# Hymba decoder layer on one core: a wide last block of the expert down part, and another order of the closing stage

## The chip, the core and the metric

The kernel runs on one core of a Trainium2 chip. The time is device microseconds of one execution, from runs of the whole kernel; lower is better. In the profile, PE is TensorE's matmuls (PEld its weight loads), DVE is VectorE, ACT is ScalarE, POOL is GpSimd, SP is SyncE, which here only issues DMA.

## The reference

One decoder layer over 256 tokens of width 2048, all in float32:

```python
h = x + concat(forgetting_attention(...), gelu(gate) * rg_lru(...)) @ w_out
hn = rms_norm(h, ffn_norm)                    # top-1 of 4 groups, top-2 of 8 experts in it
for e in range(32):
    hid = silu(hn @ w_gate[e]) * (hn @ w_up[e])          # 2048 -> 256
    out += (hid @ w_down[e]) * comb[:, e:e+1]            # 256 -> 2048
h = h + out
gate = sigmoid(rms_norm(h, ple_norm) @ w_ple_gate)       # 2048 -> 2048
h = h + gate * (p @ w_ple_up)
```

## The kernel before

A float32 matmul whose result must be close is done as three matmuls of fp32r halves: ScalarE copies a 128x512 chunk to its high half (`uh`, L179), VectorE subtracts to the low half (`ul`, L180), and TensorE sums high by high, high by low and low by high.

**Weights** stream from HBM through a ring of slots of 1 MB each (`slot()`, three pools, 12 slots in the last stages). SyncE issues the transfers in program order; each waits until its slot's last reader is through. Where a weight is an expert's, SyncE first loads the expert's number from a table (L965).

**Experts, first part.** Tokens are sorted by expert. A 0/1 matrix `sel01` (two halves of 256 sorted places, written by `select(0)` and `select(1)`, L836 to L843) gathers their rows on TensorE (`gather`, L859 and L860), and `stage1` (L900) multiplies by gate and up weights. A loop over i = 0 to 15 (L1043) takes the four experts whose slots were filled ahead: step i gathers piece i + 1, copies it, and runs stage 1 on piece i; i = 0 to 7 need the first half of `sel01`, i = 8 to 15 (whose first gather runs in step 7) the second. In between VectorE sorts the experts (`by_rank`, `by_count`). GpSimd subtracts for the splits of h (L577). Then seven rounds of four experts follow, bound by the transfer of w_gu.

**Experts, second part, with the closing gate.** Output columns come in BLOCKS of 512, 512, 512, 256 and 256. For each block, nine rounds r of two or four experts: `down(r, b)` fetches their w_down columns (one transfer for each expert, L966), multiplies (`y`, L970), copies y to `yh` (L974) and subtracts to `yl` (L975); `scatter` (L981) sums it into `o`, one round behind. After a block `o` is added to h (L1211), h is transposed (L1129) and split into `th`, `tl` (L1133, L1134), and squares are summed (L1138). In the next block's even rounds a `gate_step(b - 1, n)` multiplies these columns by chunk n of w_ple_gate (w_pg; L1174 to L1176) and adds to z (L1183). After the last block four gate steps remain, of two 128-row pieces each. The closing steps of a tile are the sigmoid on ScalarE (L1186), the product with u = p @ w_ple_up (L1187), the sum with h (L1188), and the store (L1189); for n = 0 and 1 GpSimd takes product and sum, for n = 2 and 3 VectorE.

**Order.** In this last stage SyncE and TensorE follow program order (`manual_schedule`); the scheduler orders VectorE and ScalarE.

Of the kernel before, what the change touches and what calls it, by code (L numbers as in the profile page):

```python
# [10 lines left out]
F32 = mybir.dt.float32  # L11
# [28 lines left out]
BLOCKS = ((0, 512), (512, 512), (1024, 512), (1536, 256), (1792, 256))  # L40
# [22 lines left out]
def hymba_layer_kernel(ctx, tc, x, xT, gains, w_in, w_f, rnn_v, w_gates, qk_g, b_f, w_out,  # L63
# [980 lines left out]
    for i in range(16):  # L1044
# [15 lines left out]
        if i == 0:  # L1060
            by_rank()
        elif i == 1:
            by_rank_rest()
        elif i == 2:
            token_weights()
        elif i == 3:
            token_weights_rest()
        elif i < 8:
            next(counts, None)
        if i == 6:  # L1070
            select(1)
            for r in range(pairs, 2 * pairs):
                offs[r] = offsets(r)
            masks = slot_masks(0)
        if i == 7:
            todo.append(finish(0, masks))
# [8 lines left out]
    for r in range(2 * pairs, last + 1):  # L1085
        banks[r] = s1_bank(r)
        if r > 2 * pairs:
            todo.append(finish(r - 1, masks))
        for g in range(8):
# [15 lines left out]
        masks = slot_masks(r)  # L1105
    order.close()
    order.enter_context(tc.manual_schedule(engines={mybir.EngineType.SP, mybir.EngineType.PE}))
    for _ in parts:
        pass
    gath.close()  # L1110
# [8 lines left out]
    def gate_block(b):  # L1119
# [3 lines left out]
        for a in range(0, cn // P, 2):  # L1123
            ps = bank(p_t, "t")
            pair = range(min(2, cn // P - a))
            for j in pair:
# [3 lines left out]
            for j in pair:  # L1130
# [13 lines left out]
    def gate_chunk(b, n):  # L1144
        kn = BLOCKS[b][1] // P * 512
# [3 lines left out]
        if kn > 1024:  # L1149
            return chunk(w_pg[b][n])  # L1150
        if n % 2 == 0:
            two[:] = [slot()]
            nc.sync.dma_start(two[0][:, :2 * kn].rearrange("p (n f) -> p n f", n=2),
                              w_pg[b][n:n + 2].rearrange("n p f -> p n f"))
        return two[0][:, (n % 2) * kn:(n % 2 + 1) * kn]

    def gate_step(b, n, th, tl, w, pre=()):
        kn = BLOCKS[b][1] // P
        final = b == end and n == 3
        if final:  # L1160
            units = [split_unit(w[:, j * 512:(j + 1) * 512]) for j in range(kn)]
        pool, tag = (p_s1, "s1") if n % 2 == 0 else (p_t, "t")
        parts = [(tb, 0, 512, bank(pool, tag)) for tb in range(2)]
        if final:
            parts[1:] = [(1, 0, 256, parts[1][3]), (1, 256, 256, bank(p_y, "y"))]
        for j, (tb, c0, cn, ps) in ([(j, q) for q in parts for j in range(kn)] if final else
                                    [(j, q) for j in range(kn) for q in parts]):
            if not final and tb == 0:
                uh, ul = pre[j] if j < len(pre) else split_unit(w[:, j * 512:(j + 1) * 512])
            elif final:  # L1170
                uh, ul = units[j]
            cs = slice(tb * P, (tb + 1) * P)
            o, a, c = ps[:, :cn], uh[:, c0:c0 + cn], ul[:, c0:c0 + cn]
            nc.tensor.matmul(o, th[:, j, cs], a, start=j == 0, stop=False)  # L1174
            nc.tensor.matmul(o, th[:, j, cs], c, start=False, stop=False)
            nc.tensor.matmul(o, tl[:, j, cs], a, start=False, stop=j == kn - 1)  # L1176
        for tb, c0, cn, ps in parts:
            cs = slice(n * 512 + c0, n * 512 + c0 + cn)
            zz = z[:, tb, cs]
            if b == 0:  # L1180
                nc.scalar.activation(zz, ps[:, :cn], AF.Copy)
            else:
                nc.vector.tensor_tensor(zz, zz, ps[:, :cn], ALU.add)  # L1183
            if b == end:
                eng = nc.vector if final or (n == 2) else nc.gpsimd
                nc.scalar.activation(zz, zz, AF.Sigmoid, scale=rstd3[:, tb:tb + 1])  # L1186
# [249 lines left out]
```

## Time and profile before

| | us |
|---|---|
| median of 3 runs (lowest, highest) | 941.59 (941.31, 941.66) |
| profiled execution, its own time | 941.37 |
| its span, first to last instruction | 939.6 |
| TensorE busy in the span | 840.2 (89%) |
| VectorE busy | 448.2 (48%) |
| ScalarE busy | 360.9 (38%) |
| GpSimd busy | 80.0 (9%) |
| chain that ended last | PE 65%, DMA 23%, DVE 7%, ACT 2% |

Up to 360 us the kernel projects and attends; to 475 it sorts and gathers; to 690 it runs the first part of the experts, to 905 the second, and then the closing. A busy share is an average over these stages. In the chain, the first part of the experts is a wait for w_gu, the second mostly matmuls. HBM is read for 284.85 MB.

### The profile page before, as it was taken

The page shows a single profiled execution, that of the slowest core. Times are in us where ns is not written, and L with a number is a line of the kernel's source. Part 1 is how long each engine was busy: PE and PEld are TensorE (multiplying, and loading weights), DVE is VectorE, ACT ScalarE, POOL GpSimd, SP SyncE. Part 2 cuts the span into 40 slices and gives each one's busy share as a digit, 9 for nine tenths or more (in the row PEclk, how much of TensorE's full clock was granted, in tenths as well). Part 3 has the DMA queues.
Part 4 walks back from the last instruction along what each step waited for, and adds up shares of the span by engine and source line. Part 5 has one row for each costly group of instructions (what it writes and reads, how often), then busy time and mean ns, then how long its engine had stood idle before and what let it go on. Part 6 is the DMA issues. An engine that isn't in the chain of part 4 may idle for free.

```text
span 939.6 us, 14433 instructions
## 1 busy us (share of the span) xinstructions
PE 840.2 (89%) x4627; PEld 534.4 (57%) x4627; DVE 448.2 (48%) x1110; ACT 360.9 (38%) x814; POOL 80.0 (9%) x127
## 2 busy tenths in 40 slices
PE   9999999999999999989877676678688999999973
PEld 8999877778878777544422121133122455566652
DVE  7578787675575544572312131023101324454557
ACT  6686876565565543324110000024001424242333
POOL 0000011000100002233211011010100000000005
PEclk9999999999999999999998889989898999999987
DMA  9955453534559846569999999989999999999842
GB/s 321 426 197 185 175 180 137 179 135 175 185 224 372 359 177 231 203 255 353 413 424 426 426 426 426 424 340 426 426 419 417 418 418 418 419 359 318 291 155 93
DMA packets 57875, 290.06 MB, mean 309 GB/s; under 512 B 6848, under 2 KB 7744, under 8 KB 32320
## 3 DMA queue, kind: packets, MB, share of 16 engines
q1 hardware_dynamic: 56816, 286.55, 77.7%
q10 hardware_dynamic: 976, 2.52, 0.7%
q8 instruction: 39, 0.64, 0.3%
q14 instruction: 44, 0.36, 0.1%
HBM read 284.85 MB, written 4.19 MB: 308 GB/s over the span
## 4 chain that ended last, share of the span: by engine, by line
PE 65%; DMA 23%; DVE 7%; ACT 2%; issue 1%; POOL 0%; SPq 0%; DVEq 0%; ACTq 0%
DMA wchunk<-w_gu 17%; PE s L900 7%; PE y L970 5%; PE acc L221 4%; PE acc L219 4%; DMA wchunk<-w_dn 4%; PE acc L220 4%; PE o L981 3%; PE acc L206 3%; PE acc L205 3%; PE acc L204 3%; PE y L900 2%; PE t L545 2%; PE t L546 2%; PE s L1174 2%; PE acc L451 2%
## 5 line engine op out<-in xcount | busy, mean ns | idle before, releaser
L180 DVE TENSOR_TENSOR ul<-wchunk,uh 128x512 fp32r<-128x512 f32 x296 | 199.8, 693 | 109.9 <-ACT uh L179 109.0
L900 PE MATMUL s<-wchunk,xs 128*32 128x512 f32 (+1 forms) x896 | 176.2, 662 | 62.1 <-DMA wchunk<-w_gu 53.1
L179 ACT ACTIVATE uh<-wchunk 128x512 fp32r<-128x512 f32 x296 | 180.3, 628 | 133.0 <-PE acc L221 47.6
L900 PEld LDWEIGHTS s<-wchunk,xs 128*32 128x32 f32 (+1 forms) x896 | 49.0, 121 | 166.8 <-issue 137.5
L970 PE MATMUL y<-wchunk,store 128*32 128x512 f32 (+3 forms) x640 | 82.5, 526 | 2.7 <-DMA wchunk<-w_dn 1.7
L219 PE MATMUL acc<-uh,xh 128*128 128x512 f32 x192 | 77.1, 401 | 0.0
L220 PE MATMUL acc<-ul,xh 128*128 128x512 f32 x192 | 76.8, 400 | 0.0
L221 PE MATMUL acc<-uh,xl 128*128 128x512 f32 x192 | 76.3, 397 | 0.0
L204 PE MATMUL acc<-xh,uh 128*128 128x256 f32 x256 | 72.0, 282 | 0.6 <-ACT uh L179 0.6
L206 PE MATMUL acc<-xh,ul 128*128 128x256 f32 x256 | 71.4, 279 | 0.5 <-DVE ul L180 0.5
L205 PE MATMUL acc<-xl,uh 128*128 128x256 f32 x256 | 71.6, 280 | 0.0
L974 ACT ACTIVATE yh<-y 128x512 fp32r<-128x512 f32 (+1 forms) x45 | 23.0, 511 | 125.7 <-PE y L970 125.7
L975 DVE TENSOR_TENSOR yl<-y,yh 128x512 fp32r<-128x512 f32 (+1 forms) x45 | 26.2, 582 | 92.9 <-ACT yh L974 92.7
L936 ACT ACTIVATE sg<-s,sc 128x256 f32<-128x256 f32 x8 | 3.8, 474 | 133.5 <-DVE sc L920 133.5
L920 DVE COPY sc<-t 128x2 f32<-128x2 f32 x10 | 1.6, 159 | 107.2 <-PE t L918 107.2
L891 DVE COPY xs<-xsT 128x64 f32 (+1 forms) x224 | 31.4, 210 | 40.9 <-PE s L900 25.9
L204 PEld LDWEIGHTS acc<-xh,uh 128*128 128x128 f32 x256 | 48.0, 188 | 0.9 <-ACT uh L179 0.8
L206 PEld LDWEIGHTS acc<-xh,ul 128*128 128x128 f32 x256 | 48.1, 188 | 0.7 <-DVE ul L180 0.7
L205 PEld LDWEIGHTS acc<-xl,uh 128*128 128x128 f32 x256 | 48.1, 188 | 0.3 <-DVE xl L125 0.2
L970 PEld LDWEIGHTS y<-wchunk,store 128*32 128x32 f32 (+1 forms) x640 | 21.5, 113 | 44.5 <-issue 27.9
L910 POOL TENSOR_SCALAR q<-iota,d 128x128 f32<-128x128 f32 x40 | 25.4, 649 | 205.6 <-PE t L918 174.8
L219 PEld LDWEIGHTS acc<-uh,xh 128*128 128x128 f32 x192 | 36.1, 188 | 8.7 <-ACT uh L179 0.4
(396 smaller groups left out, 1348.4 us busy)
## 6 DMA issues: line engine op xcount, KB each, us to landing
wchunk<-w_gu SPq DMA_DIRECT2D x128, 1024.0 KB, 13.3
wchunk<-w_dn SPq DMA_DIRECT2D x96, 512.0 KB, 10.6
wchunk<-w_in SPq DMA_DIRECT2D x37, 1024.0 KB, 4.8
wchunk<-w_out SPq DMA_DIRECT2D x16, 1024.0 KB, 6.8
wchunk<-w_pg SPq DMA_DIRECT2D x16, 1024.0 KB, 8.8
wchunk<-w_dn SPq DMA_DIRECT2D x64, 256.0 KB, 5.0
wchunk<-w_in SPq DMA_DIRECT2D x12, 256.0 KB, 5.9
h<-x SPq DMA_DIRECT2D x2, 1024.0 KB, 13.1
```

The costliest lines, as they stand in the source:

```text
L179: nc.scalar.activation(uh, raw, AF.Copy)
L180: nc.vector.tensor_tensor(ul, raw, uh.bitcast(F32), ALU.subtract)
L204: nc.tensor.matmul(o, uh[:, cs], a, start=first, stop=False)
L205: nc.tensor.matmul(o, uh[:, cs], b, start=False, stop=False)
L206: nc.tensor.matmul(o, ul[:, cs], a, start=False, stop=last)
L219: nc.tensor.matmul(ps[tb], a[:, c], uh, start=kt == 0, stop=False)
L220: nc.tensor.matmul(ps[tb], a[:, c], ul, start=False, stop=False)
L221: nc.tensor.matmul(ps[tb], b[:, c], uh, start=False, stop=kt == KT - 1)
L891: nc.vector.tensor_copy(to, src)
L900: nc.tensor.matmul(s1[i * width:(i + 1) * width, :], xs[:, j, i * width:(i + 1) * width], w[:, k:k + 512], start=kt == 0, stop=kt == KT - 1)
L970: nc.tensor.matmul(y[i * width:(i + 1) * width, :cn], store[f][:, first + i * width:first + (i + 1) * width], w[:, f, :], start=f == 0, st ...
L981: nc.tensor.matmul(o[tb][:, :yy.shape[1]], scat[p][:, tb * P:(tb + 1) * P], yy, start=p + i == 0, stop=p + i == len(ROUNDS))
```

## The change

- BLOCKS are four of 512 columns. The last is gated in four steps of four pieces; `slots` no longer serve two steps with one chunk.
- VectorE and ScalarE keep program order to the end too (the second `order.close()` is gone).
- `select(1)` stands in step i = 2 in place of 6. The masks of a round (`slot_masks`, GpSimd) are asked for inside the round; the last stage-1 round's `finish` is spread over r = 1 to 5 of block 0.
- In an even round two of the four splits stand ahead of y and two in the middle of the gate step.
- In the last block w_pg chunks 0 and 1 of the final gate are fetched after r = 5 and r = 7 and split at once into two ring slots each (`slot_split`: the slot leaves the ring until the gate step has read it). A 128x2 sigmoid (`warm`) loads ScalarE's table after r = 3. Gate step 3 of block 2 surrounds the last scatter.
- In the end each tile's sum, sigmoid, product, sum and store stand together (`post`), all on VectorE and ScalarE, with a pair of splits of chunk 2 or 3 ahead of it in steps 0 and 1.

```diff
-BLOCKS = ((0, 512), (512, 512), (1024, 512), (1536, 256), (1792, 256))
+BLOCKS = ((0, 512), (512, 512), (1024, 512), (1536, 512))
...
             token_weights()
+            select(1)
...
         if i == 6:
-            select(1)
             for r in range(pairs, 2 * pairs):
                 offs[r] = offsets(r)
-            masks = slot_masks(0)
         if i == 7:
-            todo.append(finish(0, masks))
+            todo.append(finish(0, slot_masks(0)))
...
+            if masks is None and g == {2 * pairs: 7, 2 * pairs + 1: 4}.get(r, 1):
+                masks = slot_masks(r)
     for _ in parts:
         pass
+    todo.append(finish(last, masks))
+    step()
...
+            ps = bank(p_y, "y") if b == end else bank(p_t, "t")
...
+        return chunk(w_pg[b][n])
...
+    def gate_step(b, n, t, units, w, mid=None):
         pool, tag = (p_s1, "s1") if n % 2 == 0 else (p_t, "t")
-        parts = [(tb, 0, 512, bank(pool, tag)) for tb in range(2)]
-        if final:
-            parts[1:] = [(1, 0, 256, parts[1][3]), (1, 256, 256, bank(p_y, "y"))]
-        for j, (tb, c0, cn, ps) in ([(j, q) for q in parts for j in range(kn)] if final else
-                                    [(j, q) for j in range(kn) for q in parts]):
-            if not final and tb == 0:
-                uh, ul = pre[j] if j < len(pre) else split_unit(w[:, j * 512:(j + 1) * 512])
-            elif final:
-                uh, ul = units[j]
-            cs = slice(tb * P, (tb + 1) * P)
-            o, a, c = ps[:, :cn], uh[:, c0:c0 + cn], ul[:, c0:c0 + cn]
-            nc.tensor.matmul(o, th[:, j, cs], a, start=j == 0, stop=False)
-            nc.tensor.matmul(o, th[:, j, cs], c, start=False, stop=False)
-            nc.tensor.matmul(o, tl[:, j, cs], a, start=False, stop=j == kn - 1)
-        for tb, c0, cn, ps in parts:
-            cs = slice(n * 512 + c0, n * 512 + c0 + cn)
-            zz = z[:, tb, cs]
+        ps = [bank(pool, tag) for _ in range(2)]
+        for a in range(2):
+            for j in range(2 * a, 2 * a + 2):
+                for tb in range(2):
+                    gate_mm(ps[tb], t, tb, j, units[j], j == 0, j == 3)
+            if a == 0:
+                units += units_of(w, range(2, 4))
+                if mid is not None:
+                    mid()
...
-            if b == end:
-                eng = nc.vector if final or (n == 2) else nc.gpsimd
-                nc.scalar.activation(zz, zz, AF.Sigmoid, scale=rstd3[:, tb:tb + 1])
-                eng.tensor_tensor(zz, zz, u[tb][:, cs], ALU.mult)
-                eng.tensor_tensor(zz, zz, h[:, tb, cs], ALU.add)
-                nc.sync.dma_start(out[tb * P:(tb + 1) * P, cs], zz)
...
+    def slot_split(w):
+        pair = []
+        for _ in range(2):
+            lent.append(slots.popleft())
+            pair.append(lent[-1].tile([P, 4, 512], F32R, tag="w", name="half"))
+        for j in range(4):
+            raw, uh, ul = w[:, j * 512:(j + 1) * 512], pair[0][:, j, :], pair[1][:, j, :]
+            nc.scalar.activation(uh, raw, AF.Copy)
+            nc.vector.tensor_tensor(ul, raw, uh.bitcast(F32), ALU.subtract)
+            if j % 2:
+                yield [(pair[0][:, k, :], pair[1][:, k, :]) for k in range(j + 1)]
...
+            n = r // 2 - 1 if b > 0 and r % 2 == 0 else None
+            if n is not None:
+                w = gate_chunk(b - 1, n)
+                units = units_of(w, range(2))
...
             nxt = down(r, b)
             scatter(o, *ready)
             ready = nxt
-            if step:
-                gate_step(b - 1, r // 2 - 1, *t, w, pre)
-            if b == 0 and r == 2:
-                for _ in finish(last, masks):
+            if n is not None and not (b == end and n == 3):
+                for _ in gate_step(b - 1, n, t, units, w):
                     pass
+            if b == 0 and todo:
+                step()
+            if b == end and r in (5, 7):
+                split[r // 2 - 2] = all_of(slot_split(gate_chunk(end, r // 2 - 2)))
+            if b == end and r == 3:
+                nc.scalar.activation(warm, rstd2, AF.Sigmoid)
...
+    def last_rows():
         scatter(o, *ready)
-        for tb in range(2):
-            hs = h[:, tb, c0:c0 + cn]
-            nc.vector.tensor_tensor(hs, hs, o[tb][:, :cn], ALU.add)
-        if b < end:
-            ready = down(0, b + 1)
-        t = gate_block(b)
-    ws = [gate_chunk(end, n) for n in range(4)]
+        add_rows(o, end)
+
+    left = gate_step(end - 1, 3, t, units, w, last_rows)
+    next(left)
+    late = [gate_chunk(end, n) for n in range(2, 4)]
+    t = gate_block(end)
+    next(left)
+
+    def post(n, tb, ps, c0, cn):
+        cs = slice(n * 512 + c0, n * 512 + c0 + cn)
+        zz = z[:, tb, cs]
+        nc.vector.tensor_tensor(zz, zz, ps[:, :cn], ALU.add)
+        nc.scalar.activation(zz, zz, AF.Sigmoid, scale=rstd3[:, tb:tb + 1])
+        yield
+        nc.vector.tensor_tensor(zz, zz, u[tb][:, cs], ALU.mult)
+        nc.vector.tensor_tensor(zz, zz, h[:, tb, cs], ALU.add)
+        nc.sync.dma_start(out[tb * P:(tb + 1) * P, cs], zz)
+
+    coming = None
     for n in range(4):
-        gate_step(end, n, *t, ws[n])
+        pool, tag = ((p_s1, "s1"), (p_t, "t"), (p_y, "y"), (p_o, "o"))[n]
+        if n < 2:
+            coming = slot_split(late[n])
+        for tb in range(2):
+            for c0, cn in (((0, 512),) if (n, tb) != (3, 1) else ((0, 256), (256, 256))):
+                ps = bank(pool, tag) if c0 == 0 else bank(p_s1, "s1")
+                for j in range(4):
+                    gate_mm(ps, t, tb, j, split[n][j], j == 0, j == 3, slice(c0, c0 + cn))
+                if n < 2:
+                    split[n + 2] = next(coming)
+                done = post(n, tb, ps, c0, cn)
+                next(done)
+                for _ in done:
+                    pass
+        for _ in range(2):
+            slots.append(lent.pop(0))
```

**VectorE, the selection.** In the difference of the two orders, at the places of i = 2 and i = 6 (`sel` is `sel01`, `pos` the sorted places, L871 the evacuation of a gather):

```order
 L704 TENSOR_SCALAR gn<-asg 128x64
 L705 TENSOR_TENSOR rank_bc<-gn,rks 128x64
+L839 TENSOR_SCALAR pos_2887<-pos_2887 128x4
+L842 TENSOR_SCALAR sel_4046<-xsT_3969,pos_2887 128x256
+L843 SCALAR_TENSOR_TENSOR sel_4046<-xsT_3969,pos_2887,sel_4046 128x256
+L842 TENSOR_SCALAR sel_4047<-xsT_3969,pos_2887 128x256
+L843 SCALAR_TENSOR_TENSOR sel_4047<-xsT_3969,pos_2887,sel_4047 128x256
 L871 TENSOR_SCALAR xsT_4026<-t,gain_sb 128x256
```

```order
 L754 TENSOR_SCALAR tri<-tri 128x32
 L755 SCALAR_TENSOR_TENSOR tri<-tri 128x32
-L839 TENSOR_SCALAR pos_2887<-pos_2887 128x4
-L842 TENSOR_SCALAR sel_4046<-xsT_3969,pos_2887 128x256
-L843 SCALAR_TENSOR_TENSOR sel_4046<-xsT_3969,pos_2887,sel_4046 128x256
-L842 TENSOR_SCALAR sel_4047<-xsT_3969,pos_2887 128x256
-L843 SCALAR_TENSOR_TENSOR sel_4047<-xsT_3969,pos_2887,sel_4047 128x256
```

Five instructions move from behind the counting of i = 6 to behind the token weights of i = 2.

**VectorE, the closing.** Before, from the last sum with h on (`z` the gate's sums, `t`, `s`, `y`, `o` PSUM banks):

```order
L1211 TENSOR_TENSOR h<-h,o 128x256 x2
L1140 TENSOR_REDUCE rstd_6875<-ss_6874 128x2
L1134 SCALAR_TENSOR_TENSOR tl<-t,gain_sb,th 128x256 x2
L180 TENSOR_TENSOR ul<-wchunk,uh 128x512
L1183 TENSOR_TENSOR z<-z,s_10102 128x512
L1183 TENSOR_TENSOR z<-z,s_10103 128x512
L180 TENSOR_TENSOR ul<-wchunk,uh 128x512
L1183 TENSOR_TENSOR z<-z,t 128x512 x2
L180 TENSOR_TENSOR ul<-wchunk,uh 128x512 x2
```

Now, from the same point (`half` is a split chunk in a lent slot; L1245, L1248, L1249 are a tile's sum, product and sum):

```order
L1202 TENSOR_TENSOR h<-h,o 128x512 x2
L1134 SCALAR_TENSOR_TENSOR tl<-y,gain_sb,th 128x256 x4
L1140 TENSOR_REDUCE rstd_6881<-ss_6880 128x2
L1178 TENSOR_TENSOR z<-z,t 128x512 x2
L1189 TENSOR_TENSOR half<-wchunk,half 128x512 x2
L1245 TENSOR_TENSOR z<-z,s_9548 128x512
L1248 TENSOR_TENSOR z<-z,u 128x512
L1249 TENSOR_TENSOR z<-z,h 128x512
L1189 TENSOR_TENSOR half<-wchunk,half 128x512 x2
L1245 TENSOR_TENSOR z<-z,s_9572 128x512
L1248 TENSOR_TENSOR z<-z,u 128x512
L1249 TENSOR_TENSOR z<-z,h 128x512
```

A tile's three steps now follow each other, the product right behind the sum that ScalarE's sigmoid reads.

**SyncE, the last block's transfers.** Before, around the chunk for the final gate's steps 0 and 1 (the second number is a transfer's columns):

```order
L1153 DMA wchunk<-w_pg 128x2x1024
L965 TENSOR_LOAD sorted_id
L965 ISA x2
L966 ISA
L966 DMA wchunk<-w_dn 128x512
```

Now:

```order
L966 DMA wchunk<-w_dn 128x1024
L83 DMA wchunk<-w_pg 128x2048 x2
L965 TENSOR_LOAD sorted_id
L965 ISA x2
L966 ISA
L966 DMA wchunk<-w_dn 128x1024
```

Two w_pg transfers stand together now (a chunk of the final gate and one of block 2), and a down transfer has twice the columns.

## Rows read from the trace of the kernel before

**Rows 1.** The page, 40 slices of the span: what the DMA engines moved, GB/s.

```profile
GB/s 321 426 197 185 175 180 137 179 135 175 185 224 372 359 177 231 203 255 353 413 424 426 426 426 426 424 340 426 426 419 417 418 418 418 419 359 318 291 155 93
```

**Rows 2.** Timeline of TensorE's matmuls around i = 6 and 7: start us, us, engine, line, tile, shapes, count, and in brackets the idle time before with what ended it.

```profile
407.54 0.39 PE L859 MATMUL o<-sel,hh 128*128 128x256 f32 x1
...
408.69 3.65 PE L900 MATMUL s<-wchunk,xs 128*64 128x512 f32 x16
415.51 0.45 PE L859 MATMUL t<-sel,hh 128*128 128x256 f32 x1 [3.17 <-DVE sel L843]
...
417.87 4.24 PE L900 MATMUL s<-wchunk,xs 128*64 128x512 f32 x16
```

**Rows 3.** Timeline of VectorE, behind i = 2's work and at i = 6, same columns.

```profile
398.31 0.48 DVE L871 TENSOR_SCALAR xsT<-t,gain_sb 128x256 f32<-128x256 f32 x1 [4.02 <-ACT xsT L869]
...
412.71 1.34 DVE L842 TENSOR_SCALAR sel<-xsT,pos 128x256 fp32r<-128x256 f32 x1
414.09 1.37 DVE L843 SCALAR_TENSOR_TENSOR sel<-xsT,pos,sel 128x256 fp32r<-128x256 f32 x1
415.38 0.34 DVE L842 TENSOR_SCALAR sel<-xsT,pos 128x256 fp32r<-128x256 f32 x1
```

**Rows 4.** Timeline of GpSimd, same columns.

```profile
394.52 2.51 POOL L577 TENSOR_TENSOR hl<-h,hh 128x512 fp32r<-128x512 f32 x2 [10.41 <-ACT hh L576]
...
412.65 2.52 POOL L577 TENSOR_TENSOR hl<-h,hh 128x512 fp32r<-128x512 f32 x2
```

**Rows 5.** Windows of 2 us: stretch, its length, busy us (instructions) of PE, PEld, DVE, ACT and POOL, the clock granted to TensorE, the busy share of the DMA engines, GB/s.

```profile
428.00:430.00 2.00, 2.00 (x14) 1.15 (x14) 0.57 (x3) 1.02 (x3) 2.00 (x4) 1.00 0.71 299
430.00:432.00 2.00, 2.00 (x12) 0.57 (x8) 0.77 (x3) 0.44 (x2) 0.64 (x3) 1.00 0.46 66
432.00:434.00 2.00, 2.00 (x16) 1.38 (x14) 0.00 (x0) 0.19 (x1) 0.00 (x0) 1.00 0.70 287
```

**Rows 6.** Windows of the second part of the experts, same columns.

```profile
735.00:785.00 50.00, 50.00 (x263) 28.21 (x263) 16.48 (x27) 18.64 (x35) 0.00 (x0) 1.00 1.02 419
785.00:835.00 50.00, 50.00 (x267) 28.58 (x266) 22.57 (x37) 18.90 (x37) 0.00 (x0) 1.00 1.02 409
835.00:900.00 65.00, 63.45 (x465) 42.97 (x463) 36.77 (x67) 22.24 (x53) 0.00 (x0) 1.00 0.90 301
```

**Rows 7.** Waits of SyncE's queue from 780 to 818 us: line and what it waited for, us in total, times, longest us.

```profile
SPq L966 <- DMA wchunk<-w_pg: 3.7, 3, 1.3
SPq L83 <- DMA wchunk<-w_dn: 3.4, 3, 1.6
```

**Rows 8.** The same from 825 to 900 us (all there are).

```profile
SPq L966 <- PE t L1176: 0.3, 1, 0.3
SPq L83 <- DMA wchunk<-w_dn: 0.3, 1, 0.3
SPq L966 <- DMA wchunk<-w_dn: 0.2, 1, 0.2
```

**Rows 9.** Timeline of SyncE's queue: start us, us from the first issue to the end of the last, line, count.

```profile
812.83 10.25 SPq L966 DMA_DIRECT2D wchunk<-w_dn  x8
...
865.06 17.63 SPq L966 DMA_DIRECT2D wchunk<-w_dn  x16
```

**Rows 10.** Timeline of TensorE: y of the last round.

```profile
900.22 1.05 PE L970 MATMUL y<-wchunk,store 128*32 128x256 f32 x10 [0.93 <-DMA wchunk<-w_dn]
```

**Rows 11.** Timeline of ScalarE in the closing.

```profile
905.12 2.19 ACT L179 ACTIVATE uh<-wchunk 128x512 fp32r<-128x512 f32 x4 [3.43 <-DMA wchunk<-w_pg]
...
910.53 0.47 ACT L1133 ACTIVATE th<-t,gain_sb 128x256 fp32r<-128x256 f32 x1 [0.24 <-PE t L1129]
911.55 0.47 ACT L1133 ACTIVATE th<-t,gain_sb 128x256 fp32r<-128x256 f32 x1 [0.55 <-DVE tl L1134]
...
917.45 0.72 ACT L1186 ACTIVATE z<-z,rstd 128x512 f32<-128x512 f32 x1
```

**Rows 12.** Timeline of VectorE in the closing.

```profile
911.03 0.48 DVE L1134 SCALAR_TENSOR_TENSOR tl<-t,gain_sb,th 128x256 fp32r<-128x256 f32 x1 [0.55 <-ACT th L1133]
...
926.47 3.42 DVE L1187 TENSOR_TENSOR z<-z,u 128x512 f32<-128x512 f32 x2
...
933.06 0.82 DVE L1187 TENSOR_TENSOR z<-z,u 128x256 f32<-128x256 f32 x2 [0.25 <-ACT z L1186]
933.81 0.76 DVE L1188 TENSOR_TENSOR z<-z,h 128x256 f32<-128x256 f32 x2
```

**Rows 13.** The chain that ended last, at the end of block 2: start us, us, engine, tile, line, count.

```profile
824.26 1.85 PE y L970 x16
827.24 2.46 PE y L970 x16
829.69 1.13 PE o L981 x4
```

**Rows 14.** The same chain, one matmul of a gate step.

```profile
744.48 0.23 PE s L1174
```

**Rows 15.** Line 966, 780 to 818 us: from issue to landing, us.

```profile
DMA to landing us min/median/max: 9.9/11.2/12.1
```

**Rows 16.** Timeline of TensorE: the eight transposes of a block.

```profile
788.46 1.09 PE L1129 MATMUL t<-ident,h 128*128 128x128 f32 x8
```

**Rows 17.** Timeline of ScalarE: a square of a block.

```profile
787.19 0.63 ACT L1138 ACTIVATE jk<-h 128x512 bf16<-128x512 f32 x1 [0.82 <-DVE h L1211]
```

## What I predict, blind

> **What bounds the kernel now.** I read the page's slices first, then the windows of the last stages, then the waits of SyncE's queue, and the timelines at the two places where the slices show a hole. From slice 20 on DMA moves some 420 GB/s in nearly every slice up to 835 us [rows 1]: the stream of expert weights hardly breaks, so whatever starts it earlier ends the kernel earlier, and what TensorE, VectorE or ScalarE do beside it is covered. Two places are not covered.
>
> The first is the start of that stream. At 412.3 us TensorE stops for 3.17 us, for the second half of the selection matrix, and the matmuls behind the stop are slower: the gather takes from 415.51 to 417.87, where the one before took from 407.54 to 408.69, and the next 16 expert matmuls 4.24 us, where the same 16 took 3.65 [rows 2]. VectorE writes that half only from 412.5 on, and its first two operations last 1.34 and 1.37 us, the third 0.34 [rows 3]; GpSimd's subtraction runs beside the first two [rows 4]. DMA idles a little later, between 428 and 434 us [rows 5], because ring slots come free only as TensorE reads them; after that it stays at work.
>
> The second is the end. Over 735 to 835 us DMA moves 419 and 409 GB/s; over 835 to 900 us, where the down weights come in 256-column transfers of 256 KB, only 301 GB/s, at a busy share of 0.90 [rows 6]. Earlier, SyncE's queue waits for transfers in front of it [rows 7]; in the narrow blocks it waits 0.8 us in 75 us [rows 8] and needs 17.63 us to issue 16 transfers, where 8 of double size take 10.25 [rows 9]. So no slot is missing there: issuing at 1.1 us for each 256 KB is the limit (238 GB/s; the w_pg chunks between them lift it to 301). TensorE feels it at 900.22, where it waits 0.93 us for the last down weights [rows 10], and ScalarE at 905.12, 3.43 us for w_pg [rows 11]. From the last down weight to the end of the span pass 939.6 - 900.2 = 39.4 us. VectorE's two products at 926.47 last 3.42 us there, two of half the width later 0.82 [rows 12].
>
> **The earlier selection.** `select(1)` moves from i = 6 to i = 2, to where VectorE stands idle for 4.02 us before 398.31. There it takes 0.16 + 1.34 + 1.37 + 0.34 + 0.48 = 3.7 us (the two ends estimated from their neighbours [rows 3]) if GpSimd's operation at 394.52 [rows 4] slows it as the one at 412.65 does now: from 394.3 to 398.0, just in time. TensorE then goes from 412.3 straight into the gather (1.15 us) and starts the expert matmuls at 413.5 at the faster pace: 417.87 - 413.5 = 4.4 us, and 0.6 for the slow ones, 5.0 in all. If the selection ends a little late I lose 0.3. I take 4.9; the bounds are 0 (the stream starts no earlier for a reason I don't see) and 5.2. That DMA follows is read from rows 5: its last idle time ends with an issue that TensorE's reads release.
>
> **The wide last block.** Columns 1536 to 2047 come as 32 transfers of 512 KB in place of 64 of 256 KB. In blocks 1 and 2 TensorE and DMA are level: the last y group of block 2 lasts 2.46 us in place of 1.85 [rows 13], so its fourth expert lands near 828.5, with TensorE waiting. From there to the last down weight of the new block 3 come 16 MB of it, the four w_pg chunks of block 2, and two of block 3, which are now fetched behind r = 5 and r = 7: 22 chunks of 1.049 MB. At 419 GB/s that is 2.50 us each, 55.1 us. TensorE's own work there is less: nine rounds of 1.85 + 1.13 [rows 13] and three gate steps of 24 matmuls at 0.23 [rows 14], 5.6 us each, are 43.6. So DMA binds the block, and the last weight lands at 828.5 - 4.9 + 55.1 = 878.7, against 900.2: 21.5 us earlier. If DMA runs ahead by what TensorE leaves (the early chunks then cost nothing) it is 5.6 us less; if the block keeps 301 GB/s, 22 chunks take 76.6 us, 21.5 more. I take 419, since the transfers have the shape of those it was measured with. The Trainium skill (DMA: Bandwidth & Descriptors, section Bandwidth) gives 341 GB/s for a 1 MB transfer and asks for at least that size, which speaks against 512 KB ones. By it the 22 chunks take 67.6 us and the sum rises by 12.5; the 512 KB transfers of rows 6, queued one behind the other at 419, do not bear it out.
>
> Slots: four ring slots are lent to the split chunks (two at r = 5, two at r = 7), so 12 shrink to 10 and 8. Counted through, the tightest transfer is the first of round 8, which takes the slot of chunk 0: that is split some 6 us after it lands, and the transfer should be issued about 9 us after (it lands 8 chunks, 20 us, later, and landing takes 11.2 [rows 15]). So I cost the lending at 0, with 3 us to spare; each further 1 us late is 1 us on the sum.
>
> The hand-written order puts two splits ahead of y's copy and two behind it. After y ends ScalarE needs 0.6 for the copy and 0.6 for each split, VectorE 0.69 and 0.62 for each behind it; the third split is ready about 2.0 us after y, the fourth 2.65, and TensorE wants them at 1.13 + 2.8 = 3.9 and 5.3. Covered; I take 0, up to 3 us over all steps.
>
> **The closing.** TensorE, from the last weight: five matmuls (1.15), scatter 1.13, half of gate step 3 (2.78), the last scatter 1.13, the other half 2.78: 9.0 us to a point T0. Behind that VectorE is the bound, by its order: it does every tile's add, product and sum itself, and stands still during the sigmoid. First the transposes (half of 1.09 [rows 16]) and four pairs th, tl that take turns on a bank, as from 910.53 to 911.55 [rows 11, 12]: tl ends at T0 + 4.1, ScalarE's two squares (0.63 each [rows 17], with the reads of their sums an estimated 1.5) at 5.0, the reduction at 5.2, the two z sums held back at 6.5, two splits at 7.8. A tile then costs 0.69 (add) + 0.72 (sigmoid [rows 11]) + 0.62 + 0.69 = 2.75 with handovers (full width estimated from the halves of rows 12), and 4.0 with the two splits that four of the seven full tiles carry. T0 + 7.8 + 2.75 = 10.55; three tiles of 4.0: 22.55; three of 2.75: 30.8; two halves of 1.7: 34.2. TensorE is through at about T0 + 24 and hides behind it. From VectorE's last sum to the end of the span: 934.57 to 939.6, 5.0 us [rows 12]. So 9.0 + 34.2 + 5.0 = 48.2 us against 39.4: 8.8 longer. A few per cent on VectorE's steps are 2 us either way; were TensorE the bound after all, the closing would be 7 us shorter.
>
> **Sum.** -21.5 + 8.8 = -12.7 on a span of 939.6: 926.9. The profiled execution itself took 941.37, 1.77 more than its span, so 928.7; the median of the runs shown is 0.2 above it: 929.
>
> **Rivals.**
> - TensorE bounds the wide block: the early chunks are hidden by its slack, T0 comes 5.6 us sooner, 923. For it: the two are nearly level. Against it: the stretched group at 827.24. 12%.
> - VectorE does not bound the closing (its handovers overlap): up to 7 us, 922. The order stands against it. 8%.
> - The early selection does not move the stream: 934. 8%.
> - Splits or lent slots make TensorE or the queue wait several us: 932 to 939. 10%.
> - Half of the wide transfers run like the narrow ones: 11 chunks at 301 and 11 at 419 GB/s are 65.9 us, 10.8 more, 940, no change. The Trainium skill's figure (DMA: Bandwidth & Descriptors, Bandwidth) would come out near here. 2%.
> - Slower: what held DMA at 301 GB/s was missing slots, and lending four makes it no better; 929 + 21.5 = 950. It decides once the block's rate is under some 340 GB/s (12.7 us lost in 22 chunks). Rows 8 speak against it, since the queue did not wait. 6%.
>
> My forecast, 929 with 924 to 934 around it, has 54%. About 0.2% (940 to 943 are no change) is what a measurement can tell. Faster: all but the last two and a piece of the fourth, 0.89; same 0.04; slower 0.07. Range 921 to 939: it leaves out the two last rivals and little else.
>
> **What would show it.** No stop at 412 us, and DMA idle for the last time near 427. Over 830 to 875 us a rate near 419 GB/s and SyncE waiting again. TensorE's last wait for down weights near 878, the chain on VectorE from about 893 on with ScalarE's sigmoids between, its last sum near 922. The prediction is wrong if DMA idles in block 3, or if TensorE stands at the end of the chain.

## The result, and the profile after

The changed kernel takes 929.89 us (median of 4 runs, 927.63 to 934.18), beside 941.62 (4 runs) for the kernel before: a ratio of 0.9872, 95% interval [0.9828, 0.9917], 1.3% faster. The forecast was 929. The profiled execution took 928.82 us, its span is 927.1.

The start of the stream. TensorE's timeline at the place of [rows 2], with the same columns: the gather of the second half follows the expert matmuls at once.

```profile
409.53 3.65 PE L900 MATMUL s<-wchunk,xs 128*64 128x512 f32 x16
413.11 0.39 PE L859 MATMUL t<-sel,hh 128*128 128x256 f32 x1
...
414.25 3.65 PE L900 MATMUL s<-wchunk,xs 128*64 128x512 f32 x16
```

The stop of 3.17 us is gone, and the matmuls behind it last 3.65 us and not 4.24. VectorE's selection stands at i = 2 now:

```profile
395.25 0.35 DVE L842 TENSOR_SCALAR sel<-xsT,pos 128x256 fp32r<-128x256 f32 x1
395.63 1.38 DVE L843 SCALAR_TENSOR_TENSOR sel<-xsT,pos,sel 128x256 fp32r<-128x256 f32 x1
396.94 1.36 DVE L842 TENSOR_SCALAR sel<-xsT,pos 128x256 fp32r<-128x256 f32 x1
398.33 0.48 DVE L843 SCALAR_TENSOR_TENSOR sel<-xsT,pos,sel 128x256 fp32r<-128x256 f32 x1
```

Two of the four operations are slow, as two were in [rows 3]. The windows of [rows 5] come next, and then those of [rows 6], with the same columns; DMA's last gap lies between 426 and 430 us, not 428 to 434:

```profile
426.00:428.00 2.00, 2.00 (x12) 0.51 (x8) 0.56 (x3) 0.24 (x2) 0.43 (x3) 1.00 0.74 201
428.00:430.00 2.00, 2.00 (x16) 1.41 (x16) 0.00 (x0) 0.40 (x1) 0.00 (x0) 1.00 0.84 336
430.00:432.00 2.00, 2.00 (x12) 0.69 (x10) 0.85 (x3) 1.45 (x5) 0.26 (x1) 1.00 1.02 422
```

```profile
735.00:785.00 50.00, 49.91 (x263) 28.33 (x263) 17.66 (x29) 20.33 (x39) 0.00 (x0) 1.00 1.02 418
...
835.00:860.00 25.00, 25.00 (x138) 13.80 (x136) 12.52 (x21) 10.60 (x22) 0.00 (x0) 1.00 1.02 419
860.00:880.00 20.00, 19.19 (x87) 8.49 (x84) 11.88 (x19) 9.06 (x17) 0.00 (x0) 1.00 0.98 408
```

The last block runs at 419 and 408 GB/s, where it ran at 301. SyncE's queue waits again in 825 to 880 us, in place of the 0.8 us of [rows 8]. Its five longest waits (what issued, for what, us in total, times, longest):

```profile
SPq L966 <- DMA wchunk<-w_pg: 5.9, 4, 2.1
SPq L83 <- DMA wchunk<-w_dn: 4.4, 5, 0.9
SPq L966 <- DMA wchunk<-w_dn: 2.5, 9, 0.9
SPq L966 <- DVE ul L180: 2.3, 1, 2.3
SPq L966 <- DVE half L1189: 1.1, 1, 1.1
```

The last two are waits for a split, one of them into a lent slot; DMA stayed at 408 to 419 GB/s beside them. TensorE's last matmuls on down weights (which stood at 900.22 us in [rows 10]), and the last transposes:

```profile
877.78 1.05 PE L970 MATMUL y<-wchunk,store 128*32 128x512 f32 x2 [0.23 <-DMA wchunk<-w_dn]
879.04 1.90 PE L970 MATMUL y<-wchunk,store 128*32 128x512 f32 x10 [0.22 <-DMA wchunk<-w_dn]
...
888.42 1.03 PE L1129 MATMUL y<-ident,h 128*128 128x128 f32 x8
```

VectorE in the closing, which answers to [rows 12]: the last `tl`, the reduction, one tile with its splits, the last sum.

```profile
892.00 0.48 DVE L1134 SCALAR_TENSOR_TENSOR tl<-y,gain_sb,th 128x256 fp32r<-128x256 f32 x1 [0.54 <-ACT th L1133]
893.37 0.16 DVE L1140 TENSOR_REDUCE rstd<-ss 128x2 f32<-128x8 f32 x1 [0.88 <-ACT jk L1138]
...
898.71 1.29 DVE L1189 TENSOR_TENSOR half<-wchunk,half 128x512 fp32r<-128x512 f32 x2
899.91 0.68 DVE L1245 TENSOR_TENSOR z<-z,s 128x512 f32<-128x512 f32 x1
901.38 0.69 DVE L1248 TENSOR_TENSOR z<-z,u 128x512 f32<-128x512 f32 x1 [0.79 <-ACT z L1246]
902.11 0.69 DVE L1249 TENSOR_TENSOR z<-z,h 128x512 f32<-128x512 f32 x1
...
922.41 0.43 DVE L1249 TENSOR_TENSOR z<-z,h 128x256 f32<-128x256 f32 x1
```

From its add to the next tile's add, such a tile takes 4.0 us (899.91 to 903.92), of which VectorE stands idle for 0.79 us, waiting for the sigmoid.

### The profile page after: what moved, and what is told of

It reads as the page before. It is cut to its first block, busy times and chain, and to the rows that moved or that the text cites. A ratio compares the mean times of both kernels' runs of the same rounds, so it can differ in the third digit from the quotient of the medians.

```text
span 927.1 us, 13858 instructions
## 1 busy us (share of the span) xinstructions
PE 836.5 (90%) x4469; PEld 524.9 (57%) x4469; DVE 441.9 (48%) x1099; ACT 358.9 (39%) x802; POOL 67.6 (7%) x119
## 4 chain that ended last, share of the span: by engine, by line
PE 53%; DMA 37%; DVE 5%; ACT 2%; issue 1%; SPq 1%; POOL 0%; DVEq 0%; ACTq 0%
DMA wchunk<-w_dn 18%; DMA wchunk<-w_gu 16%; PE s L900 9%; PE acc L221 4%; PE acc L219 4%; PE acc L220 4%; PE acc L206 3%; PE acc L204 3%; PE acc L205 3%; PE y L900 2%; PE t L545 2%; PE t L546 2%; PE acc L450 2%; PE acc L451 2%; PE acc L452 2%; PE t L547 2%
## 5 line engine op out<-in xcount | busy, mean ns | idle before, releaser
L180 DVE TENSOR_TENSOR ul<-wchunk,uh 128x512 fp32r<-128x512 f32 x280 | 188.9, 689 | 100.4 <-ACT uh L179 99.9
L179 ACT ACTIVATE uh<-wchunk 128x512 fp32r<-128x512 f32 x280 | 171.8, 627 | 118.7 <-PE acc L221 46.9
L970 PE MATMUL y<-wchunk,store 128*32 128x512 f32 (+1 forms) x512 | 85.3, 600 | 1.8 <-DMA wchunk<-w_dn 1.5
L975 DVE TENSOR_TENSOR yl<-y,yh 128x512 fp32r<-128x512 f32 x36 | 24.9, 692 | 80.6 <-ACT yh L974 80.6
L974 ACT ACTIVATE yh<-y 128x512 fp32r<-128x512 f32 x36 | 21.4, 595 | 100.7 <-PE y L970 100.7
L204 PEld LDWEIGHTS acc<-xh,uh 128*128 128x128 f32 x256 | 48.1, 188 | 2.0 <-ACT uh L179 1.6
L205 PEld LDWEIGHTS acc<-xl,uh 128*128 128x128 f32 x256 | 48.1, 188 | 0.9 <-DVE xl L125 0.8
L206 PEld LDWEIGHTS acc<-xh,ul 128*128 128x128 f32 x256 | 48.1, 188 | 0.5 <-DVE ul L180 0.4
L970 PEld LDWEIGHTS y<-wchunk,store 128*32 128x32 f32 (+1 forms) x512 | 17.9, 112 | 49.3 <-issue 31.1
L221 PEld LDWEIGHTS acc<-uh,xl 128*128 128x128 f32 x192 | 36.1, 188 | 8.3
```

Of the source, the lines that this page charges most:

```text
L179: nc.scalar.activation(uh, raw, AF.Copy)
L180: nc.vector.tensor_tensor(ul, raw, uh.bitcast(F32), ALU.subtract)
L204: nc.tensor.matmul(o, uh[:, cs], a, start=first, stop=False)
L205: nc.tensor.matmul(o, uh[:, cs], b, start=False, stop=False)
L206: nc.tensor.matmul(o, ul[:, cs], a, start=False, stop=last)
L221: nc.tensor.matmul(ps[tb], b[:, c], uh, start=False, stop=kt == KT - 1)
```

## Experiments

Profiles of one kernel differ by some us ahead of the last block, so two lengths are compared within each trace. The last block (with the narrow blocks: the last two) goes from the end of the last `y` of block 2 to the end of the last `y` of all (a row's start and length give its end), and the closing from there to the end of the span. Before, the block is 829.7 [rows 13] to 901.27, 71.6 us, and the closing to 939.6, 38.3 us. After, the last `y` of block 2 is

```profile
822.21 2.45 PE L970 MATMUL y<-wchunk,store 128*32 128x512 f32 x16
```

so the block is 824.66 to 880.94, 56.3 us, and the closing to 927.1, 46.2 us. The first four runs (again to halves_one_load) were timed beside each other; the later ones are set against the 929.72 us of **again**, and the kernel before took 942.28 to 942.83 beside all of them.

**again.** The changed kernel, unaltered.

> The changed kernel a second time, unaltered, as the base of the runs beside it and to see what spreads its runs (927.6 to 934.2 us). If the forecast's sum is a property of the kernel, the profiled span has the last down weight near 879 us, T0 (TensorE through with gate step 3) near 888.6, VectorE's last sum at T0 + 34.2, within 0.5 us each, and the median is 927 to 932. If the spread comes from the clock granted to TensorE, a profile with another mean clock than 0.968 differs from the first in the first part of the experts (475 to 735 us) and not in the last block, where DMA binds (55 us for 22 chunks), and not in the closing, where VectorE binds.

929.72 us (928.04 to 930.23); last down weight at 880.1, last block 56.3 us and closing 46.2 us as in the first profile. The shift of 1.1 us between the two profiles came from ahead of the block: this one leads by 0.9 us at 470 us and trails by 1.0 at 736. So the two part in the first part of the experts. That the clock does it is not shown: the mean clocks are 0.970 and 0.968.

**late_selection.**

```diff
         elif i == 2:
             token_weights()
-            select(1)
 ...
         if i == 6:
+            select(1)
```

> The changed kernel with the second selection half back in step i = 6. By my account the stream of weights starts later: TensorE stops some 3 us near 412, DMA idles last near 432 and not 428, and everything behind comes 4.9 us later (4 to 5.2): some 4.9 us above the changed kernel beside it. By the rival (the selection does not move the stream) it is within 1 us of it.

935.04 us (6 runs), 5.3 above the changed kernel beside it. The stop and DMA's gap are back; a row of TensorE's timeline, and a row of the windows:

```profile
415.40 0.39 PE L859 MATMUL t<-sel,hh 128*128 128x256 f32 x1 [3.17 <-DVE sel L843]
```

```profile
430.00:432.00 2.00, 2.00 (x12) 0.64 (x10) 0.97 (x4) 0.51 (x2) 0.88 (x3) 1.00 0.20 33
```

The ratios to the kernel before are 0.9911 [0.9894, 0.9928], and 0.9857 [0.9839, 0.9874] for the changed kernel, so the difference is clear; its size is known to some 2 us, and the 4.9 of the first account lies in it. The rival falls.

**halves_two_loads, halves_one_load.** In the last block each expert's transfer is issued as two halves (`k` = 0, 1), with the expert's number loaded for each half or once.

```diff
+            for k in range(2 if b == len(BLOCKS) - 1 else 1):
...
                 ex = nc.sync.value_load(sorted_id[0:1, j:j + 1], ...)   # one load: for k == 0 alone
-                nc.sync.dma_start(both[:, i % per, :], w_dn[b][ds(ex, 1)]...)
+                nc.sync.dma_start(both[:, i % per, part], w_dn[b][ds(ex, 1)]...[:, part])
```

> The changed kernel with each expert's 512 KB of the last block as two transfers of 256 KB, each with its own load of the expert's number, so that SyncE issues what it issued before for that shape; slots, splits, TensorE's work and the closing are the changed kernel's. By my account SyncE's issue binds the block: 64 x 1.1 us and six w_pg issues are 74 to 75 us in place of 55, the last down weight lands 19 to 20 us later, near 898, the queue waits under 3 us in the block, and the time is 946 to 951. If the price of an issue were hidden by transfers already queued (rival), the block stays at 419 GB/s and the time within 2 us of the changed kernel.

> As the run with two loads, but the expert's number is loaded once for both halves of 256 KB. If what costs 1.1 us is mostly the load of the number and the work on registers (of which the second transfer is now free), a pair takes 1.5 us, 32 pairs and six w_pg issues some 52 us, under the 55 of DMA: within 2 us of the changed kernel. If the 256 KB transfer itself is what runs at 301 GB/s (rival: size, not issue), the block takes 76.6 us here too and the time is 948 to 951, as with two loads.

With two loads 946.13 us, 16.4 above the changed kernel beside it (some 19 expected), with one 938.17, 8.4 above it (under 2 expected by the one account, 18 to 21 by the other, so neither holds). SyncE's issues (start, us, count), first with two loads, then with one:

```profile
842.19 17.67 SPq L969 DMA_DIRECT2D wchunk<-w_dn  x16
```

```profile
838.30 14.09 SPq L969 DMA_DIRECT2D wchunk<-w_dn  x16
```

Two loads bring back the 1.1 us for each 256 KB of [rows 9], in a kernel that has everything else of the change: the narrow transfer alone takes the whole gain away, and 3.8 us more (942.34 for the kernel before beside it). The last block takes 74.6 us with two loads and 64.4 with one, in place of 56.3. The transfers of the two runs are the same, so the 10.2 us between them come from the 32 loads of a number that SyncE does without. The page's rows of the w_dn transfers (KB each, median us from issue to landing) agree, for two loads, one load and the changed kernel:

```profile
wchunk<-w_dn SPq DMA_DIRECT2D x64, 256.0 KB, 4.8
```

```profile
wchunk<-w_dn SPq DMA_DIRECT2D x64, 256.0 KB, 6.0
```

```profile
wchunk<-w_dn SPq DMA_DIRECT2D x128, 512.0 KB, 11.0
```

A narrow transfer lands in about half the time (5.0 us in the kernel before), so less is queued in front of it: with two loads the DMA engines wait for SyncE. With one load a pair takes 1.76 us, where I had put 1.5. 32 pairs are 56.4 us, above the 55 of DMA before the w_pg issues are counted, so the second issue still costs. But the queue waits there too, between 830 and 900 us:

```profile
SPq L969 <- DMA wchunk<-w_pg: 6.0, 5, 1.8
```

And the windows of 835 to 860 us, two loads and then one, raise another question:

```profile
835.00:860.00 25.00, 23.78 (x112) 12.48 (x109) 10.28 (x17) 9.92 (x20) 0.00 (x0) 1.00 0.81 264
```

```profile
835.00:860.00 25.00, 24.85 (x132) 13.43 (x128) 11.68 (x19) 10.14 (x21) 0.00 (x0) 1.00 0.96 340
```

With one load the DMA engines are busy for 0.96 of the time and move 340 GB/s; before it was 301 at 0.90 [rows 6]. Is it the piece of 2 KB that is slow?

**halves_by_row, pieces_2k.** Two ways to separate piece, size and issue: halves by partitions (64 with 4 KB each), and one issue of 512 KB whose pieces in the slot are 2 KB, because two experts lie interleaved there.

```diff
-            nc.sync.dma_start(both[:, i % per, :], w_dn[b][ds(ex, 1)]...)
+            for ps in (slice(0, 64), slice(64, P)):             # halves_by_row, last block
+                nc.sync.dma_start(both[ps, i % per, :], w_dn[b][ds(ex, 1)]...[ps])
```

```diff
-            nc.sync.dma_start(both[:, i % per, :], w_dn[b][ds(ex, 1)].rearrange("a p f -> p (a f)"))
+            gaps = ...rearrange("p (k i f) -> p k i f", k=2, f=512)[:, :, i % per, :]   # pieces_2k
+            nc.sync.dma_start(gaps, w_dn[b][ds(ex, 1)].rearrange("a p (k f) -> p (a k) f", k=2))
```

> The changed kernel with each expert's 512 KB of the last block as two transfers of 256 KB again, the number loaded once, but cut across partitions: 64 partitions with 4 KB each, where halves_one_load had 128 with 2 KB each. If the length of a row's piece (2 or 4 KB) is what cost halves_one_load its 8.4 us (DMA share 0.94 to 0.99 at 330 to 371 GB/s there), the block runs near 419 GB/s and the time is within 2 us of the changed kernel. If the second issue (0.5 us a pair, 1.76 us for both halves) or the size of a transfer costs it, the time is 936 to 939 again.

> The changed kernel with each expert's last-block transfer still one issue of 512 KB over 128 partitions, but written into the slot as two pieces of 2 KB per partition that do not touch (the other expert's lie between), so that the transfer's packets are 2 KB as before and SyncE issues no more than the changed kernel does. If the piece is what costs halves_one_load its 8.4 us (its window shows 963 of a thousand of the engines' time for 10.37 MB, 44.6 us of one engine per MB, where the changed kernel needs 38.9), 16.8 MB cost 8 to 11 us more: 938 to 941. If the second issue costs it, this run is within 2 us of the changed kernel at 929.7.

pieces_2k takes 930.44 us, within 1 us of the changed kernel, and its last block 57.8 us, 1.6 more. That its packets were shorter shows in the totals of the DMA view for 840 to 870 us, the changed kernel first, then pieces_2k:

```profile
DMA packets 2883, 12.58 MB, mean 419 GB/s; under 512 B 322, under 2 KB 322, under 8 KB 2376
```

```profile
DMA packets 4866, 12.29 MB, mean 410 GB/s; under 512 B 317, under 2 KB 317, under 8 KB 4384
```

So the piece costs 2 to 3% of the rate, 1.6 us of the block; the other 6.5 us of halves_one_load go with its second issue. A DMA share of 0.96 did not mean full engines. Why one load costs 8.4 us and not the 5 or 6 that 56.4 us and six w_pg issues would make is not settled: the pieces and the 6.0 us of waits have a part in it, how large was not separated.

halves_by_row missed both accounts: 974.45 us, 44.7 above the changed kernel.

```profile
855.00:875.00 20.00, 14.02 (x50) 4.40 (x49) 4.43 (x7) 4.87 (x8) 0.00 (x0) 0.83 1.02 231
```

231 GB/s at a full share: transfers over 64 partitions run at little more than half the rate, so this cut could not tell piece from size. The Trainium skill (SBUF — State Buffer, section "Door 1: The DMA port swizzle") says that partitions 0 to 63 reach eight of the 16 ports and partitions 64 to 127 the other eight. The 231 beside 418 GB/s agrees. Here the engines are the limit and not SyncE, and a transfer of the same 256 KB lands late:

```profile
wchunk<-w_dn SPq DMA_DIRECT2D x64, 256.0 KB, 10.7
```

**wide_block_only.** The kernel before, with one line changed.

```diff
-BLOCKS = ((0, 512), (512, 512), (1024, 512), (1536, 256), (1792, 256))
+BLOCKS = ((0, 512), (512, 512), (1024, 512), (1536, 512))
```

> The kernel before with only its BLOCKS changed to four of 512 columns: its own scheduler's order, selection at i = 6, GpSimd in the closing, and the last gate's four chunks of 1 MB fetched and split behind the last weights. By my account the block itself gains what it does in the changed kernel: 16 MB and four w_pg chunks at 419 GB/s, the last down weight some 21 us earlier than 900.2, near 878 to 880. The closing takes TensorE 48 matmuls (11.1 us) and VectorE and ScalarE 8 splits more than the 39.4 us of before: 50 to 56 us, so the time is 931 to 937, and the new closing order (48.2) is worth 2 to 7 us. By the rival (the new order of the closing gains nothing) the closing is 45 to 48 us and the time 925 to 929, below the changed kernel by what the closing lacks.

929.23 us (926.71 to 930.99): as fast as the whole change. Its last `y`, and the end of its closing on GpSimd and VectorE:

```profile
878.78 2.71 PE L970 MATMUL y<-wchunk,store 128*32 128x512 f32 x16
```

```profile
909.40 1.61 POOL L1188 TENSOR_TENSOR z<-z,h 128x512 f32<-128x512 f32 x1
```

```profile
908.37 4.88 DVE L180 TENSOR_TENSOR ul<-wchunk,uh 128x512 fp32r<-128x512 f32 x3 [0.20 <-ACT uh L179]
```

Three splits take 4.88 us beside GpSimd, where three cost 1.9 at 867.72, with GpSimd idle; still its closing is 881.49 to 926.7, 45.2 us, 1.0 less than that of the changed kernel. My 50 to 56 was wrong, the rival's 45 to 48 right (its 925 to 929 by 0.2 us not). All that the change does beside the wide block is worth nothing in sum. But the selection alone is worth some 5 us, so the remainder costs as much: late_selection, which is the change without it, is 5.8 us slower than wide_block_only. The last block shows where: 51.3 us here, 56.3 in the changed kernel, which fetches two w_pg chunks more in it.

**overlap_tiles, overlap_early.** What VectorE's order in the closing costs.

```diff
                 next(done)
-                for _ in done:
+                for _ in behind:          # the tile before: product, sum, store
                     pass
+                behind = done
...
```

overlap_early has, besides, `split[2] = all_of(slot_split(late[0]))` ahead of the last `gate_block`, so that the tiles carry only the splits of chunk 3.

> The changed kernel with a tile's product, sum and store issued one tile later, behind the next tile's sum, so that VectorE does not stand still during the sigmoid; no instruction added or removed. By my account VectorE bounds the closing and its waits for the sigmoid there (6.7 us, nine times) go: VectorE's last sum at T0 + 27.5 in place of 34.2, the time 6 to 7 us under the changed kernel (929.7 in the last job), 922.5 to 924. By the rival (TensorE or the stores bound the closing) under 1 us. TensorE ends at T0 + 23.8, so it is not the bound yet.

> As overlap_tiles, and the four splits of w_pg chunk 2 stand ahead of the last transposes, where VectorE stands idle for 2.67 us (886.9 to 889.6 in the profile of the changed kernel), instead of in the first tiles. By my account VectorE's work behind T0 falls by another 2.5 us, and TensorE becomes the bound: its last half tile at T0 + 23.8, then sum, sigmoid, product and sum 1.9: VectorE's last sum at T0 + 25.7, the time 8 to 9 us under the changed kernel, 920.5 to 922. If the splits delay th and tl by 1 to 2 us (rival), it is 922 to 924, no better than overlap_tiles.

924.65 us and 923.95, 5.1 and 5.8 under the changed kernel (6 to 7 and 8 to 9 expected). Closings: 881.69 to 922.1, 40.4 us, and 885.05 to 924.3, 39.3. So VectorE bounded the closing; 5.8 of the 6.7 us of waits went. In overlap_tiles a new wait has come, behind the first tile's add, where no earlier tile is there to work on:

```profile
898.64 1.29 DVE L1189 TENSOR_TENSOR half<-wchunk,half 128x512 fp32r<-128x512 f32 x2 [1.37 <-ACT half L1188]
```

overlap_early gained 1.1 us more in the closing and not 2.5 (the 0.7 us between the two medians is inside the spread of its runs, 921.35 to 926.00): this wait stayed, 1.38 us, and now TensorE is waited for too. Its rival, that the splits delay `th` and `tl`, had the time, 922 to 924, but not the cause: the first `tl` starts 4.0 us after the sum with h in both runs.

```profile
913.92 0.69 DVE L1246 TENSOR_TENSOR z<-z,o 128x512 f32<-128x512 f32 x1 [0.75 <-PE o L1159]
```

**late_chunks, late_and_overlap.** All four chunks of the final gate are fetched behind the last down weight, and no slot is lent before it; the second run has the overlapped tiles too.

```diff
-            if b == end and r in (5, 7):
-                split[r // 2 - 2] = all_of(slot_split(gate_chunk(end, r // 2 - 2)))
...
         scatter(o, *ready)
+        split[0] = all_of(slot_split(late[0]))
         add_rows(o, end)
...
-    late = [gate_chunk(end, n) for n in range(2, 4)]
+    late = [gate_chunk(end, n) for n in range(4)]
...
+    split[1] = all_of(slot_split(late[1]))
     t = gate_block(end)
...
```

> The changed kernel without the two w_pg chunks of the final gate in the middle of the last block: all four are fetched behind the last down weight; chunk 0 is split ahead of the last sum with h and chunk 1 ahead of the last transposes, where VectorE stands idle (2.1 and 2.7 us), chunks 2 and 3 as in the changed kernel; no slot is lent before the last weight. By my account the two chunks are 5.0 us of DMA ahead of the last down weight (2 x 2.50) and buy nothing, since VectorE and not a chunk bounds the closing: from wide_block_only, which fetches them late and starts its stream 5 us later, and still had its last y at the same place. So the last weight comes 5.0 us sooner, the closing from it stays at 48.1 to 48.6 us, and the time is 924.5 to 926 (changed kernel: 929.7). By the rival the late chunks hold up the splits and so TensorE: a closing of 51 to 54 us and a time of 928 to 931.

> late_chunks with the tiles overlapped as in overlap_tiles. If both accounts hold and are independent, 5.0 us at the last weight and 5.1 to 5.6 behind it add up: 919 to 921, closing from the last weight 42.5 to 43. If one hides the other (rival: with late chunks TensorE or the chunks bound the closing), it is 923 to 926.

926.13 us and 919.88: 3.6 under the changed kernel, and 4.8 under overlap_tiles. The last `y` of block 2 and the last of all in late_chunks:

```profile
821.00 2.49 PE L970 MATMUL y<-wchunk,store 128*32 128x512 f32 x16
```

```profile
872.03 2.71 PE L970 MATMUL y<-wchunk,store 128*32 128x512 f32 x16
```

The last block takes 51.3 us there and 51.2 in late_and_overlap, in place of 56.3 and 56.2: 5.0 us less, the two transfers of 2.50. The closings are 874.74 to 920.9, 46.2 us, and 879.41 to 919.9, 40.5: to 0.1 us those of the changed kernel and of overlap_tiles, with two chunks more to fetch and split in them. The splits fill VectorE's two idle places; the second kernel's rows from the last `yl` to the first `tl`:

```profile
880.08 0.69 DVE L975 TENSOR_TENSOR yl<-y,yh 128x512 fp32r<-128x512 f32 x1 [1.84 <-ACT yh L974]
880.69 1.28 DVE L180 TENSOR_TENSOR ul<-wchunk,uh 128x512 fp32r<-128x512 f32 x2
881.89 2.49 DVE L1189 TENSOR_TENSOR half<-wchunk,half 128x512 fp32r<-128x512 f32 x4
884.29 1.28 DVE L1202 TENSOR_TENSOR h<-h,o 128x512 f32<-128x512 f32 x2
885.49 2.49 DVE L1189 TENSOR_TENSOR half<-wchunk,half 128x512 fp32r<-128x512 f32 x4
888.02 0.48 DVE L1134 SCALAR_TENSOR_TENSOR tl<-y,gain_sb,th 128x256 fp32r<-128x256 f32 x1
```

So the early chunks cost 5.0 us of the block and bought nothing; both accounts add up. The medians give 3.6 and 4.8, with runs that spread over 5 us. late_and_overlap beats both kernels: a ratio to before of 0.9759, [0.9737, 0.9782].

**kept_sums.** late_and_overlap, with the sums of block 2's gate step 3 kept in PSUM (`kept`), and each pair of splits one tile earlier. (The banks of the last steps change places, and TensorE no longer halves the last tile.)

```diff
-    next(left)            # z sums of gate step 3
...
-                    gate_mm(ps, t, tb, j, split[n][j], j == 0, j == 3, slice(c0, c0 + cn))
+                    gate_mm(kept[tb] if n == 3 else ps, t, tb, j, split[n][j], n < 3 and j == 0, j == 3)
```

> late_and_overlap, and two things less for VectorE behind T0: gate step 3 of block 2 leaves its sums in its PSUM banks and the last step of the final gate adds on to them there, so the two held-back z sums (1.27 us) are gone, and each pair of splits stands one tile earlier, so that VectorE no longer waits 1.37 us for ScalarE's second pair behind the first sigmoid. By my account, that VectorE still bounds the closing, these 2.6 us go nearly in full: from the end of the last y to the end of the span 40.6 us become 38.0 to 38.4, the time 917 to 918.5 (late_and_overlap: 919.9). By the rival (TensorE bounds it already) under 0.5 us.

920.06 us, no gain; closing 878.51 to 918.7, 40.2 us. The two sums (1.27 us) went, and VectorE's wait grew from 1.37 us to 0.36 and 1.65:

```profile
891.47 2.50 DVE L1190 TENSOR_TENSOR half<-wchunk,half 128x512 fp32r<-128x512 f32 x4 [0.36 <-ACT half L1189]
...
896.21 1.29 DVE L1190 TENSOR_TENSOR half<-wchunk,half 128x512 fp32r<-128x512 f32 x2 [1.65 <-ACT half L1189]
```

I had put the wait down to the place of one pair. But whichever pair stands behind the first sum, ScalarE copies its high halves only after the first sigmoid (894.93 to 895.65), in program order. Here neither account holds: VectorE stands idle for ScalarE's order, and no wait for TensorE shows in these tiles.

## Why the prediction was right, point by point

- **The sum.** 929 against 929.89. In the trace, the last down weight came 21.2 us earlier (21.5 in the sum) and the closing from it took 8.7 us more (8.8). Each term was met within 1 us; two errors of the closing cancel by luck.
- **The earlier selection, 4.9 us.** Shown: no stop, the faster matmuls, and 5.3 us when it is undone. VectorE finished it at 398.8 and not 398.0, only because its work ahead of it ran 0.8 us later in this profile; it then waited 0.31 us for ScalarE (L869), so the selection held up nothing, as forecast.
- **The wide last block.** Last weight at 878.7 forecast, 879.0 in the trace; 419 GB/s, queue waits back. That SyncE's issue had held the block is borne out from two sides: two loads bring 16.4 us back, 10.2 us of the block by the second load alone, and pieces of 2 KB in one issue cost 1.6 us of it. Missing slots (the slower rival) fall, since the block ran at 419 GB/s with four slots lent, and so does the rival that wide transfers run like the narrow ones. The rival that TensorE's slack hides the early chunks falls too: without them the block is 5.0 us shorter.
- **Lent slots and split order at 0.** The queue waited 2.3 and 1.1 us for splits; DMA stayed at 408 to 419 GB/s, and the last weight came 0.3 us after its forecast.
- **The closing, 48.2 us.** T0 came 9.6 us behind the last weight and not 9.0; from there `tl` took 3.9 us (4.1), the last sum 34.2 (34.2), and from it to the end of the span 4.3 (5.0): 48.1. The 0.6 too much and the 0.7 too little cancel by chance. VectorE as its bound is shown by overlap_tiles; the rival that it is not falls.
- **What I missed** changes no term of the sum: I took the two early chunks and the new order as given, and did not ask what the wide block would be without them. wide_block_only answers it. The early chunks lengthen the block by 5.0 us, which is all that the selection brings; and 46.2 us of closing are no less than the 45.2 that the old order makes with GpSimd.

## What to carry to other kernels

If a queue moves less than its rate and waits for nothing, count its issues: here the same bytes in half as many were worth 13 us by a change of one line. A fetch that is made early in a stream bound by DMA delays everything behind it by its own length (5.0 us for two chunks); leave it late where idle engines can take it up. On an engine that works in program order, put other work between an operation and the step that waits for another engine's answer to it: that alone gave 5.1 us.

## What the runs showed of the hardware

- Transfers over 64 partitions, the two halves one behind the other, ran at 231 GB/s where 128 partitions gave 418, both at a full DMA share.
- A high DMA share does not tell the rate: 0.96 at 340 GB/s with two issues to an expert, 1.04 at 407 with one, the pieces being of 2 KB in both.
- The cost of an issue by SyncE: 1.1 us with its own load of an expert's number, 1.76 us for two that share one load. Where that is the limit, a 256 KB transfer lands 4.8 to 6.0 us after its issue; where the DMA engines are, 10.7 us (64 partitions).
